# A queue of its own for the retention of a diffusion layer, and pooled differences written in place

## The chip, the cores and the metric

The kernel runs on one core of one Trainium2 chip, as one launch. The metric is the device time of that launch in microseconds (us), the median of three runs.

## What is computed

Two layers of a hybrid backbone over 256 latent tokens and 256 context tokens, 1024 channels. Each layer normalises and modulates its input, projects it once, feeds three token mixers in parallel, and merges them behind sigmoid gates; a SwiGLU block follows. Layer 0 computes all 512 tokens. Layer 1 computes its outputs for the 256 latent tokens alone and takes only keys and values from the context.

```python
def _token_mixers(hx, hc, w_in, ...):
    ux = _split_cols(hx @ w_in)
    ...
    a_x = _na_latent(ux[0], ux[1], ux[2], k_na_c, v_na_c, rpb)
    ...
    o_rx, _, _ = _bi_retention(q_rx, k_rx, v_rx, lg_f, lg_b, s_f, s_b)
    r_x = _ret_out(o_rx, ux[6], gn_g)
    p_x = _pool_mixer(ux[7], pool_w, pool_scale)
    mix_x = _merge(a_x, r_x, p_x, ux[8], ux[9], ux[10], wpa, wpb, wpc, wo)

def _ret_out(o, g, gn_g):
    mu = jnp.mean(o, axis=-1, keepdims=True)
    var = jnp.mean(jnp.square(o - mu), axis=-1, keepdims=True)
    y = _merge_heads((o - mu) * lax.rsqrt(var + GN_EPS)) * gn_g.astype(jnp.float32)
    return (jax.nn.silu(g.astype(jnp.float32)) * y).astype(g.dtype)

def _pool_mixer(u, pool_w, pool_scale):
    # four groups of 128 channels, windows of 2, 4, 8 and 16 tokens
    groups.append(mean - uf[..., sl])
    ...
    y = jnp.einsum('bngc,gcd->bngd', pooled, pool_w).reshape(b, n, POOL_WIDTH)
    return y * pool_scale

def _merge(a, r, p, ga, gb, gc, wpa, wpb, wpc, wo):
    m = (jax.nn.sigmoid(ga) * (a @ wpa) + jax.nn.sigmoid(gb) * (r @ wpb)
         + jax.nn.sigmoid(gc) * (p @ wpc))
    return m @ wo
```

## The kernel before

Everything is kept channel by channel: a tile has 128 channels as partitions and tokens along its rows. Every fp32 operand of a large product is split into a high and a low part of fp32r, and a product is three matmuls (`mm3`, L189 to L191). The weights stream in as 138 chunks of 128x1024 per layer. A chunk is loaded to `raw` (SyncE), its high part is cast on ScalarE (`hl`, L117), its low part subtracted on VectorE (`hl`, L107). Chunks are prepared up to three ahead of their use.

Engines take their instructions in the order in which the Python code writes them; nothing reorders them. Three helper loops issue the dense matmuls: `tokmajor` (values, token by token), `fm` (everything else, one PSUM tile of tag `g`, four of which exist, for each block of 128 output channels), and `branch`. `branch` does one of the three gated branches: for each of four pairs of output blocks two gate products (24 matmuls each, evicted on ScalarE with a sigmoid, L1000) and two branch products (12 matmuls each, merged with the gate on VectorE, L1004 to L1007).

Small work is woven into the dense matmuls by Python generators in three queues: `lanes["attn"]`, `lanes["pool"]` and `lanes["rope"]`. Within `fm` and `tokmajor`, `tick()` (L146) moves the first generator of each queue on by one step. In layer 0 `fm` does so every 6 matmuls of 512 columns, in layer 1 every 12 matmuls of 256 columns; `tokmajor` every 6 of 512. `drain(name)` (L158) runs what is left of a queue with no dense matmul between. `pipeline(items, stride)` (L168) turns lists of stages into such a generator, two steps for each stage: first what runs on the other engines, then what runs on TensorE.

The mixer of a layer, in order: keys and queries of the attention; its values (CV); with the attention queued, the retention's keys and queries, the pool's input `up` (CU), the retention's values `rv` (CRV), the retention's gate `gt` (CG, four blocks); then branches A (attention), C (pool) and B (retention).

The pool mixer is `pool_task` (L773). For each of four groups it makes running sums on GpSimd (`pb`, one buffer, L803 and L812), then the difference of mean and input on VectorE into a new tile `pl` (L820), then a product with `pw` on TensorE (L780), and a scaled eviction on ScalarE back into `up` (L784). It is queued when CRV begins, but a flag `hold`, set during CRV, keeps the first difference from being issued until CRV has ended. As `pb` has one buffer, the sums of the next group wait for this difference. The products come in between, through a little timetable `late`.

The retention is made of `ret_item` (L889, for each of four heads: decay tables `dm`, scores `ps`, masked scores `sm`, output `po`, statistics), `ret_stack` (L865, casts of keys `rkd`, `rkl` and queries `rqs`) and `ret_fin` (L964, normalised output `y`, its transpose `pt` on TensorE, L977, product with the gate `gt`, L980). `pt` and `po` have one PSUM tile each. All of it goes into the queue `attn`, after CG and after `drain("attn")`:

```python
        items[0][0][0]()
        items[0][1][0]()
        items[0][0] = items[0][1] = (None, None)
        lanes["attn"].append(ret_stack())
        lanes["attn"].append(pipeline(items, 4 if both else 2))
        lanes["attn"].append(pipeline([ret_fin(hd) for hd in range(4)], 2))
```

Then come four Silu on `gt` (L1044), branch A, `drain("pool")`, branch C, `drain("attn")` and branch B, which needs the finished `gt`.

Of the kernel before, what the change touches and what calls it, by code (L numbers as in the profile page):

```python
# [8 lines left out]
F32 = mybir.dt.float32  # L9
# [23 lines left out]
def hybrid_dit_kernel(ctx: ExitStack, tc: tile.TileContext, hT, wst, adaf, crow_d, vec_d,  # L33
# [52 lines left out]
        return vec[:, l * V_L + off + i:l * V_L + off + i + 1]  # L86

    raw_t, hl_t = {}, {}
    st = {"dma": 0, "prep": 0, "half": 0, "credit": 0.0, "rate": 0.0, "cap": 10 ** 6, "hold": 0, "lazy": False}
    total = 2 * NCH  # L90

    def raw_tile():
# [16 lines left out]
    def prep_to(i, wait=False):  # L109
        if not wait:  # L110
            prep_lo(i)
        while st["prep"] <= min(i, total - 1):
            j = st["prep"]
            load_to(j)
            t = wp.tile([128, 2, 1024], F32R, name="hl", tag="hl", bufs=4)
            r = raw_t.pop(j)
            S.copy(t[:, 0], r)  # L117
            late.append((j, r, t))
            if not wait:
                prep_lo(i)  # L120
            hl_t[j] = t
            st["prep"] += 1
# [9 lines left out]
        load_to(i + 5)  # L132
        flush()

    lanes = {"attn": [], "pool": [], "rope": []}
    ada_q = []

    def step(q):
        while q:
            try:  # L140
                next(q[0])
                break
            except StopIteration:
                q.pop(0)

    def tick():  # L146
        step(lanes["pool"])
# [74 lines left out]
    def chunk8(j):  # L222
        return [(j, b) for b in range(8)]
# [344 lines left out]
    def mixer(l, mp, outs, u):  # L568
# [9 lines left out]
        def t2(name):  # L578
            return mp.tile([128, 512], F32, name=name, tag="t2", bufs=5)
# [42 lines left out]
        def ev_nak(i, c=ALL):  # L622
            def ev(o):
                for a, r in enumerate(rows):
                    S.copy(nakd[2 * i + a][r, c], o[r])
                for a, r in enumerate(rows):
                    hi = nakd[2 * i + a][r, c]
                    V.tensor_tensor(nakl[2 * i + a][r, c], o[r], hi.bitcast(F32), op=ALU.subtract)
                    P.tensor_copy(nakd[2 * i + a][rows[1 - a], c], hi)
            return ev  # L630

        def ev_naq(i):
            def ev(o):
# [139 lines left out]
        def pool_task():  # L773
            pw = sm.tile([128, 4, 128], F32, name="pw", tag="acc", bufs=1)
            nc.sync.dma_start(out=pw, in_=pw_d[l])
            late = {}

            def pmm(gi, o2):
                pp = pg()
                TE.matmul(pp[:, :nq], pw[:, gi], o2[:, :nq], start=True, stop=True)  # L780
                return pp

            def pev(gi, pp):
                S.activation(up[gi][:, :, 8:264], pp[:, :nq].rearrange("p (s t) -> p s t", t=256), AF.Copy,  # L784
                             scale=vcol(l, V_PS, gi))

            t = [0]

            def pause():
                t[0] += 1  # L790
                if t[0] in late:
                    gi, o2 = late.pop(t[0])
                    pp = pmm(gi, o2)
                    late[-t[0] - 1] = (gi, pp)
                elif -t[0] in late:
                    pev(*late.pop(-t[0]))

            for gi in range(4):
                b = mp.tile([128, 1 + so, 272], F32, name="pb", tag="pb", bufs=1)
                a, w = up[gi], 1  # L800
                for j in range(gi + 1):
                    n = 272 - 2 * w + 1
                    P.tensor_tensor(b[:, :, :n], a[:, :, :n], a[:, :, w:w + n], op=ALU.add)  # L803
                    a = b
                    w *= 2
                    yield
                    pause()
                s0 = 8 - w // 2
# [13 lines left out]
                late[t[0] + 4] = (gi, o2)  # L822
                yield
                pause()
            while late:
                yield
                pause()

        if both:
            for i in range(8):  # L830
                if i == 4:
                    prep_to(10)
                (ev_nak(i) if i < 4 else ev_naq(i - 4))(outs[i])
        else:
            for i, o in enumerate(outs):
                ev_nak(i)(o)
            n = len(outs)
            fm([(chunk8(base + CK + i), ev_nak(i)) for i in range(n, 4)], hn, ALL)
            fm([(chunk8(base + CQ + i), ev_naq(i)) for i in range(4)], hn, cq)
        if both:  # L840
            decay_logs(u)
        st["lazy"] = True
        lanes["attn"].append(pipeline(items, 1, (10 if both else 0)))
        tokmajor(base + CV, hn, nav)
        fm([(chunk8(base + CRK + i), ev_k(i)) for i in range(2)], hn, ALL)
        fm([(chunk8(base + CRQ + i), ev_q(i)) for i in range(2)], hn, cq)
        fm([(chunk8(base + CU + i), ev_u(i)) for i in range(4)], hn, cq)
        drain("rope")
        lanes["pool"].append(pool_task())
        st["hold"] = 1  # L850
        tokmajor(base + CRV, hn, rv)
        st["hold"] = 0
        fm([(chunk8(base + CG + i), ev_g(i)) for i in range(4)], hn, cq)
        drain("attn")
        st["lazy"] = False

        m = [mp.tile([128, 512], F32, name=f"m{i}", tag=f"nak{i}") for i in range(4)] + nav
# [106 lines left out]
        def ret_fin(hd):  # L964
# [17 lines left out]

            return [(None, None), (norm, None), (None, trans), (fin, None)]

        def msplit(ks):
            for k in ks:
                split([t[:, cq] for t in hn[k]], m[k][:, cl])
# [44 lines left out]
                bran(0)  # L1032
                bran(1)

        items = [ret_item(hd) for hd in range(4)]
        items[0][0][0]()
        items[0][1][0]()
        items[0][0] = items[0][1] = (None, None)
# [9 lines left out]
        drain("attn")  # L1048
        branch(base + CB, [gt[i] for i in range(4)], False, True)
        if both:  # L1050
            h_tiles()
# [297 lines left out]
```

## Time and profile before

| | |
|---|---|
| median of 3 runs | 1386.01 us (1384.87 to 1386.74) |
| the profiled execution | 1382.58 us, of which 1380.8 us span of instructions |
| TensorE busy with matmuls (PE) | 1322.7 us, 96% |
| VectorE (DVE), ScalarE (ACT), GpSimd (POOL) | 894.2, 597.2, 200.2 us |
| chain that ended last | PE 87%, DVE 8%, ACT 2% |
| DMA | 207.27 MB, mean 150 GB/s |

Times in the profile are counted from the start of the span. Layer 0's mixer ends at about 430 us, layer 1's runs from about 905 to 1150 us. In a row of the timeline the number in brackets is how long the engine had been idle, and what ended the idle time. In a row of the windows view, PEclk is the share of TensorE's full clock that was granted.

### The profile page before, as it was taken

To read this page: it belongs to the slowest core of one execution; us is meant where nothing else is said; L and a number is where in the kernel's file an instruction comes from. 1 tells how busy PE (TensorE), PEld (TensorE's weight loads), DVE (VectorE), ACT (ScalarE), POOL (GpSimd) and SP (SyncE) were. 2 spreads that over 40 slices of the span, in tenths; PEclk is the share of its full clock that TensorE was granted. 3 is DMA by queue.
4 is the path that set the end of the run, shared out by engine and by line. 5 is a ranking of instruction groups with operands and counts; after the bars stand their busy time and mean duration, and the time that the engine had idled before them with its cause. 6 is when DMAs were issued, how large, how long until landed. Compare 5 with 4: busy or idle time off the path is not lost.

```text
span 1380.8 us, 19738 instructions
## 1 busy us (share of the span) xinstructions
PE 1322.7 (96%) x7658; PEld 1147.2 (83%) x7658; DVE 894.2 (65%) x1467; ACT 597.2 (43%) x929; POOL 200.2 (14%) x230
## 2 busy tenths in 40 slices
PE   4799999899999999999999999999999989999997
PEld 2578777688888888888888888988889989899997
DVE  8997554766877766565555653665538877655555
ACT  5484554544232435232123232465556545544453
POOL 6652302412000001000000000142134200000000
PEclk9999999999999999999999999999999999999999
DMA  7433322433545624355445653243435665455553
GB/s 261 168 110 117 98 71 83 128 123 122 183 162 162 201 71 138 124 171 165 155 139 172 211 183 99 70 140 108 142 122 185 217 237 177 151 184 195 183 171 106
DMA packets 62304, 207.27 MB, mean 150 GB/s; under 512 B 7041, under 2 KB 11521, under 8 KB 62209
## 3 DMA queue, kind: packets, MB, share of 16 engines
q1 hardware_dynamic: 50546, 163.97, 36.3%
q10 hardware_dynamic: 11664, 42.04, 9.2%
q8 instruction: 60, 0.98, 0.3%
q14 instruction: 34, 0.28, 0.1%
HBM read 204.94 MB, written 1.05 MB: 149 GB/s over the span
## 4 chain that ended last, share of the span: by engine, by line
PE 87%; DVE 8%; ACT 2%; issue 2%; DMA 0%; POOL 0%; SPq 0%; DVEq 0%; ACTq 0%; POOLq 0%
PE pg L189 26%; PE pg L190 26%; PE pg L191 26%; PE po L941 1%; DVE hl L107 1%; DVE tmp L441 1%; PE pt L675 1%; PE po L687 1%; DVE mods L522 1%; PE ps L643 1%; PE ps L644 1%; DVE rkl L876 0%; ACT hl L117 0%; DVE acc L476 0%; ACT hh L310 0%
## 5 line engine op out<-in xcount | busy, mean ns | idle before, releaser
L189 PE MATMUL pg<-hh,hl 128*128 128x256 f32 (+1 forms) x1568 | 530.9, 339 | 15.2 <-ACT hh L516 12.7
L191 PE MATMUL pg<-hl,hl 128*128 128x256 f32 (+1 forms) x1568 | 527.4, 336 | 2.2 <-DVE hl L542 1.6
L190 PE MATMUL pg<-hh,hl 128*128 128x256 f32 (+1 forms) x1568 | 526.2, 336 | 1.4 <-DVE hl L107 1.4
L107 DVE TENSOR_TENSOR hl<-raw,hl 128x1024 fp32r<-128x1024 f32 x276 | 342.3, 1244 | 174.8 <-ACT hl L117 169.8
L117 ACT CAST hl<-raw 128x1024 fp32r<-128x1024 f32 x276 | 287.6, 1046 | 207.5 <-PE pg L191 108.0
L189 PEld LDWEIGHTS pg<-hh,hl 128*128 128x128 f32 x1568 | 302.0, 193 | 48.7 <-ACT hh L516 15.1
L191 PEld LDWEIGHTS pg<-hl,hl 128*128 128x128 f32 x1568 | 301.7, 192 | 34.6 <-DVE hl L542 4.3
L190 PEld LDWEIGHTS pg<-hh,hl 128*128 128x128 f32 x1568 | 301.9, 193 | 32.1 <-DVE hl L107 2.1
L378 DVE CUSTOM_DVE_ANT_0 tmp<-ada,cb 128x1024 bf16<-128x1024 f32 x128 | 156.1, 1226 | 27.1 <-DMA ada<-in_adaf 17.8
L189 PE MATMUL pg<-fh,hl 128*128 128x256 f32 (+1 forms) x374 | 121.6, 325 | 0.0
L190 PE MATMUL pg<-fh,hl 128*128 128x256 f32 (+1 forms) x374 | 121.4, 325 | 0.0
L191 PE MATMUL pg<-fl,hl 128*128 128x256 f32 (+1 forms) x374 | 121.4, 325 | 0.0
L319 POOL TENSOR_TENSOR hl<-tmp,hh 128x256 fp32r<-128x256 f32 x20 | 14.8, 738 | 627.4 <-ACT hh L308 371.1
L291 ACT CAST fh<-sg 128x512 fp32r<-128x512 f32 (+1 forms) x44 | 22.6, 513 | 140.9 <-DVE sg L1150 140.9
L190 PEld LDWEIGHTS pg<-fh,hl 128*128 128x128 f32 x374 | 70.1, 188 | 7.2
L189 PEld LDWEIGHTS pg<-fh,hl 128*128 128x128 f32 x374 | 70.1, 187 | 7.1
L191 PEld LDWEIGHTS pg<-fl,hl 128*128 128x128 f32 x374 | 70.1, 187 | 7.1
L335 DVE SCALAR_TENSOR_TENSOR h<-pg,mods,h 128x256 f32<-128x256 f32 x72 | 32.7, 480 | 65.8 <-PE pg L191 65.7
L1150 DVE TENSOR_TENSOR sg<-pg,sg 128x512 f32<-128x512 f32 (+1 forms) x44 | 24.5, 557 | 51.1 <-PE pg L191 47.7
L1000 ACT ACTIVATE tmp<-pg 128x512 f32<-128x512 f32 (+1 forms) x48 | 23.5, 490 | 77.2 <-PE pg L191 76.2
L1147 ACT ACTIVATE sg<-pg 128x512 f32<-128x512 f32 (+1 forms) x44 | 21.6, 491 | 69.2 <-PE pg L191 69.2
L189 PE MATMUL pg<-hl,hh 128*128 128x512 f32 x128 | 50.6, 395 | 0.0
(241 smaller groups left out, 1643.4 us busy)
## 6 DMA issues: line engine op xcount, KB each, us to landing
raw<-in_wst SPq DMA_DIRECT2D x276, 512.0 KB, 3.6
ada<-in_adaf ACTq DMA_DIRECT2D x80, 512.0 KB, 3.8
wa<-in_adaf SPq DMA_DIRECT2D x16, 512.0 KB, 4.5
h<-in_hT SPq DMA_DIRECT2D x16, 256.0 KB, 5.0
bm<-in_bias SPq DMA_DIRECT2D x32, 128.0 KB, 2.0
out<-yt SPq DMA_DIRECT2D x4, 256.0 KB, 2.8
cs<-in_rope SPq DMA_DIRECT2D x2, 256.0 KB, 3.0
pw<-in_pw SPq DMA_DIRECT2D x2, 256.0 KB, 3.6
```

Source lines behind the costliest of these rows:

```text
L107: V.tensor_tensor(t[:, 1], r, t[:, 0].bitcast(F32), op=ALU.subtract)
L117: S.copy(t[:, 0], r)
L189: TE.matmul(o, wh, xh, start=a, stop=False)
L190: TE.matmul(o, wl, xh, start=False, stop=False)
L191: TE.matmul(o, wh, xl, start=False, stop=z)
L291: S.copy(d0, src)
L319: P.tensor_tensor(hn[k][1][:, c], t[:, c], hi, op=ALU.subtract)
L335: V.scalar_tensor_tensor(h[k][:, c], o, mods[l][:, col + k, s:s + 1], h[k][:, c], op0=ALU.mult, op1=ALU.add)
L378: V.tensor_tensor_reduce(out=tmp().bitcast(BF16), in0=tiles[n], in1=cb[s], scale=1.0, scalar=0.0, op0=ALU.mult, op1=ALU.add, accum_out=mod ...
L1000: S.activation(sg[f][:, cl], o, AF.Sigmoid)
L1147: S.activation(e["s"][:, c], o, AF.Silu)
L1150: V.tensor_tensor(e["s"][:, c], o, e["s"][:, c], op=ALU.mult)
```

## The change

There is a fourth queue, `lanes["ret"]`. `tick()` moves it on whenever the queue `attn` is empty. It holds one generator, `ret_lane`, queued at the start of CRV: the first head's decay, `ret_stack`, a wait for the end of `hold`, the heads' pipeline, a wait for a flag `gated`, then `ret_fin`. The four Silu follow `drain("attn")` directly and set `gated`. Branch B is preceded by `drain("ret")`.

The pool's difference is written into `up` itself, over its own input. `hold` no longer stands ahead of it, so sums and differences of all four groups are issued one after the other from the start of CRV, with two steps between the last sum and the difference. All four products and evictions follow when `hold` has ended, a product every second step; the timetable `late` is gone.

```diff
@@ tick
-        step(lanes["attn"])
+        step(lanes["attn"] or lanes["ret"])
@@ pool_task
+            ov = [t[:, :, 8:264] for t in up]
...
+            def pmm(gi):
                 pp = pg()
-                TE.matmul(pp[:, :nq], pw[:, gi], o2[:, :nq], start=True, stop=True)
+                TE.matmul(pp[:, :nq], pw[:, gi], ov[gi], start=True, stop=True)
                 return pp
...
-                for _ in range(4):
-                    yield
-                    pause()
-                while st["hold"]:
-                    yield
-                o2 = t2("pl")
-                ov = o2[:, :nq].rearrange("p (s t) -> p s t", t=256)
-                V.scalar_tensor_tensor(ov, b[:, :, s0:s0 + 256], 1.0 / w, up[gi][:, :, 8:264],
+                yield
+                yield
+                V.scalar_tensor_tensor(ov[gi], b[:, :, s0:s0 + 256], 1.0 / w, ov[gi],
                                        op0=ALU.mult, op1=ALU.subtract)
-                late[t[0] + 4] = (gi, o2)
                 yield
-                pause()
-            while late:
+            while st["hold"]:
                 yield
-                pause()
+            for gi in range(4):
+                pp = pmm(gi)
+                yield
+                pev(gi, pp)
+                yield
@@ mixer
+        def ret_lane():
+            items = [ret_item(hd) for hd in range(4)]
+            items[0][0][0]()
+            items[0][1][0]()
+            items[0][0] = items[0][1] = (None, None)
+            yield
+            yield from ret_stack()
+            while st["hold"]:
+                yield
+            yield from pipeline(items, 4 if both else 2)
+            while not st["gated"]:
+                yield
+            yield from pipeline([ret_fin(hd) for hd in range(4)], 2)
...
         lanes["pool"].append(pool_task())
         st["hold"] = 1
+        lanes["ret"].append(ret_lane())
         tokmajor(base + CRV, hn, rv)
         st["hold"] = 0
         fm([(chunk8(base + CG + i), ev_g(i)) for i in range(4)], hn, cq)
         drain("attn")
+        for i in range(4):
+            S.activation(gt[i], gt[i], AF.Silu)
+        st["gated"] = True
         st["lazy"] = False
...
-        lanes["attn"].append(ret_stack())
-        lanes["attn"].append(pipeline(items, 4 if both else 2))
-        lanes["attn"].append(pipeline([ret_fin(hd) for hd in range(4)], 2))
         st["rate"] = 0.75 if both else 0.45
-        for i in range(4):
-            S.activation(gt[i], gt[i], AF.Silu)
         branch(base + CA, None, True)
         drain("pool")
         branch(base + CC, [up[i][:, :, 8:264] for i in range(4)], False)
-        drain("attn")
+        drain("ret")
+        st["gated"] = False
         branch(base + CB, [gt[i] for i in range(4)], False, True)
```

How the instructions move, at three places.

TensorE in layer 0, the fourth group's product (L780; `pl` is the new tile of before, `up` the input). Before it stands behind the first pair of branch A (`naq` is the attention's output):

```order
L191 MATMUL pg<-naq_677,hl 128x512
L189 MATMUL pg<-naq_678,hl 128x512
L190 MATMUL pg<-naq_678,hl 128x512
L191 MATMUL pg<-naq_679,hl 128x512
L780 MATMUL pg<-pl,pw 128x512
L189 MATMUL pg<-hh_85,hl 128x512
L190 MATMUL pg<-hh_85,hl 128x512
```

Now, at the start of the last block of CG:

```order
L189 MATMUL pg<-hh_99,hl 128x512
L190 MATMUL pg<-hh_99,hl 128x512
L191 MATMUL pg<-hl_100,hl 128x512
L780 MATMUL pg<-up_683,pw 128x512
L189 MATMUL pg<-hh_85,hl 128x512
```

It has moved ahead of the whole first pair of branch A, and its difference on VectorE has moved from between the retention's casts (`rqs`) to well ahead of them. The retention's own matmuls stand where they stood in layer 0.

TensorE in layer 1, the retention's last transposes (L977, now L933). Before, two heads' transposes stand together (two each) at the end of branch C, ahead of branch B:

```order
L190 MATMUL pg<-br_8846,hl 128x256
L191 MATMUL pg<-br_8847,hl 128x256
L977 MATMUL pt<-ident,y 128x128 x4
L189 MATMUL pg<-hh_85,hl 128x256
L190 MATMUL pg<-hh_85,hl 128x256
```

Now only the last head's two stand there; the third head's stand 48 dense matmuls earlier:

```order
L190 MATMUL pg<-hh_99,hl 128x256
L191 MATMUL pg<-hl_100,hl 128x256
L933 MATMUL pt<-ident,y 128x128 x2
L189 MATMUL pg<-hh_85,hl 128x256
...
L191 MATMUL pg<-br_8868,hl 128x256
L933 MATMUL pt<-ident,y 128x128 x2
L189 MATMUL pg<-hh_85,hl 128x256
```

ScalarE in layer 1, from the last copy of CG's gate to the first two sigmoids of branch A (L1000, now L1003). Before (`dm` is the first head's decay, L903 to L905):

```order
L619 COPY gt_8245<-pg 128x256
L903 ACTIVATE dm<-dtab,lg_84 128x384
L904 ACTIVATE tmp<-dtab,lg_84 128x384
L905 ACTIVATE dm<-dm 128x384
L1044 ACT_TABLE_LOAD
...
L871 CAST rkd_8271<-rk_6985 64x512
L871 CAST rkd_8288<-rk_6985 64x512
L117 CAST hl<-raw 128x1024
L1000 ACT_TABLE_LOAD
L1000 ACTIVATE tmp<-pg 128x256
```

Now:

```order
L619 COPY gt_8289<-pg 128x256
L983 ACT_TABLE_LOAD
...
L841 CAST rqs<-rq_6983 64x256
L784 ACTIVATE up_7014<-pg,vec 128x256
L841 CAST rqs<-rq_6983 64x256
L117 CAST hl<-raw 128x1024
L1003 ACT_TABLE_LOAD
L1003 ACTIVATE tmp<-pg 128x256
```

The decay and the key casts have moved ahead of the last copy, into CG; two query casts and one eviction of a pool product have come in. The number of table loads is the same, 26.

## Rows read from the trace of the kernel before

**Rows 1.** The page, part 1: busy time, share of the span, instructions.
```profile
PE 1322.7 (96%) x7658; PEld 1147.2 (83%) x7658; DVE 894.2 (65%) x1467; ACT 597.2 (43%) x929; POOL 200.2 (14%) x230
```
**Rows 2.** Waits of TensorE, whole span: us in total, times, longest.
```profile
PE pt L977 <- DVE y L970: 3.8, 1, 3.8
PE pg L780 <- DVE pl L820: 3.5, 1, 3.5
PE pg L189 <- ACT tmp L1000: 3.1, 4, 1.1
PE po L941 <- DVE sm L923: 2.0, 1, 2.0
```
**Rows 3.** Timeline of TensorE, layer 0, branch A: start, us, instruction [idle before].
```profile
262.52 2.05 PE L780 MATMUL pg<-pl,pw 128*128 128x512 f32 x2 [3.54 <-DVE pl L820]
263.58 1.42 PE L189 MATMUL pg<-hh,hl 128*128 128x512 f32 x1
...
268.21 0.48 PE L189 MATMUL pg<-hh,hl 128*128 128x512 f32 x1
```
**Rows 4.** Windows: stretch, us, busy of PE, PEld, DVE, ACT, POOL; PEclk, DMA.
```profile
262.52:268.21 5.69, 5.69 (x12) 3.79 (x13) 5.16 (x7) 1.85 (x3) 0.00 (x0) 0.50 0.80 257
```
**Rows 5.** Timeline of VectorE, layer 0, the fourth group's difference.
```profile
261.68 0.69 DVE L820 SCALAR_TENSOR_TENSOR pl<-pb,up 128x512 f32<-128x512 f32 x1
```
**Rows 6.** Timeline of GpSimd: layer 0's fourth group; layer 1's third and fourth.
```profile
251.19 2.18 POOL L812 TENSOR_TENSOR pb<-pb,icnt 128x8 f32<-128x8 f32 x4
...
1026.86 0.64 POOL L803 TENSOR_TENSOR pb<-up 128x271 f32<-128x271 f32 x1
...
1043.83 3.96 POOL L803 TENSOR_TENSOR pb<-pb 128x269 f32<-128x269 f32 x3
```
**Rows 7.** Timeline of TensorE, layer 0, a pool product that did not wait.
```profile
233.74 1.02 PE L780 MATMUL pg<-pl,pw 128*128 128x512 f32 x2
...
234.82 0.39 PE L190 MATMUL pg<-hh,hl 128*128 128x512 f32 x1
235.05 0.40 PE L191 MATMUL pg<-hl,hl 128*128 128x512 f32 x1
```
**Rows 8.** Timeline of ScalarE: a gate's copy in layer 0; layer 1, CG to branch A.
```profile
236.17 0.59 ACT L619 COPY gt<-pg 128x512 f32<-128x512 f32 x1 [3.90 <-PE pg L191]
...
1024.24 0.37 ACT L619 COPY gt<-pg 128x256 f32<-128x256 f32 x1 [1.56 <-PE pg L191]
...
1026.23 1.28 ACT L1044 ACT_TABLE_LOAD   x1
1027.53 1.34 ACT L1044 ACTIVATE gt<-gt 128x256 f32<-128x256 f32 x4
1028.77 1.24 ACT L871 CAST rkd<-rk 64x512 fp32r<-64x512 f32 x2
...
1031.11 1.28 ACT L1000 ACT_TABLE_LOAD   x1
1032.41 0.38 ACT L1000 ACTIVATE tmp<-pg 128x256 f32<-128x256 f32 x1
```
**Rows 9.** Timeline of TensorE, layer 1, end of branch C and start of branch B.
```profile
1116.22 0.66 PE L977 MATMUL pt<-ident,y 128*128 128x128 f32 x2 [3.75 <-DVE y L970]
1116.53 0.56 PE L189 MATMUL pg<-hh,hl 128*128 128x256 f32 x1
...
1121.89 0.28 PE L190 MATMUL pg<-hh,hl 128*128 128x256 f32 x1
1122.01 0.28 PE L191 MATMUL pg<-hl,hl 128*128 128x256 f32 x1
```
**Rows 10.** Windows, as rows 4, layer 1, after the wait of rows 9.
```profile
1116.20:1121.90 5.70, 5.68 (x28) 5.69 (x29) 4.32 (x9) 1.41 (x3) 0.00 (x0) 0.52 0.22 70
```
**Rows 11.** Timeline of VectorE, layer 1, behind branch C's merges.
```profile
1115.34 0.48 DVE L980 SCALAR_TENSOR_TENSOR gt<-pt,vec,gt 128x256 f32<-128x256 f32 x1
1115.73 0.59 DVE L970 TENSOR_SCALAR y<-y,mv,gr 128x128 f32<-128x128 f32 x2
```

More of the change, by code (lines that the diff above doesn't have):

```diff
@@ L88, in hybrid_dit_kernel @@
     raw_t, hl_t = {}, {}
-    st = {"dma": 0, "prep": 0, "half": 0, "credit": 0.0, "rate": 0.0, "cap": 10 ** 6, "hold": 0, "lazy": False}
+    st = {"dma": 0, "prep": 0, "half": 0, "credit": 0.0, "rate": 0.0, "cap": 10 ** 6, "hold": 0, "gated": False, "lazy": False}
     total = 2 * NCH
@@ L133, in use @@
         flush()
-    lanes = {"attn": [], "pool": [], "rope": []}
+    lanes = {"attn": [], "pool": [], "rope": [], "ret": []}
     ada_q = []
@@ L775, in pool_task @@
             nc.sync.dma_start(out=pw, in_=pw_d[l])
-            late = {}
-            def pmm(gi, o2):
+            ov = [t[:, :, 8:264] for t in up]
+            def pmm(gi):
                 pp = pg()
-                TE.matmul(pp[:, :nq], pw[:, gi], o2[:, :nq], start=True, stop=True)
+                TE.matmul(pp[:, :nq], pw[:, gi], ov[gi], start=True, stop=True)
                 return pp
             def pev(gi, pp):
-                S.activation(up[gi][:, :, 8:264], pp[:, :nq].rearrange("p (s t) -> p s t", t=256), AF.Copy,
+                S.activation(ov[gi], pp[:, :nq].rearrange("p (s t) -> p s t", t=256), AF.Copy,
                              scale=vcol(l, V_PS, gi))
[L787 to L796, printed above, removed]
             for gi in range(4):
@@ L812, in pool_task @@
                         P.tensor_tensor(b[:, s, c], b[:, s, c], icnt[:, gi, e], op=ALU.mult)
-                for _ in range(4):
-                    yield
-                    pause()
-                while st["hold"]:
-                    yield
-                o2 = t2("pl")
-                ov = o2[:, :nq].rearrange("p (s t) -> p s t", t=256)
-                V.scalar_tensor_tensor(ov, b[:, :, s0:s0 + 256], 1.0 / w, up[gi][:, :, 8:264],
+                yield
+                yield
+                V.scalar_tensor_tensor(ov[gi], b[:, :, s0:s0 + 256], 1.0 / w, ov[gi],
                                        op0=ALU.mult, op1=ALU.subtract)
-                late[t[0] + 4] = (gi, o2)
                 yield
-                pause()
-            while late:
+            while st["hold"]:
                 yield
[L827 to L853, printed above, removed]
-        drain("attn")
-        st["lazy"] = False
-        m = [mp.tile([128, 512], F32, name=f"m{i}", tag=f"nak{i}") for i in range(4)] + nav
+            for gi in range(4):
[3 more added lines that the diff above has]
+                yield
         tts = range(4) if both else range(2, 4)
@@ L983, in ret_fin @@
             return [(None, None), (norm, None), (None, trans), (fin, None)]
+        def ret_lane():
[11 more added lines that the diff above has]
+            yield from pipeline([ret_fin(hd) for hd in range(4)], 2)
+        if both:
+            for i in range(8):
+                if i == 4:
+                    prep_to(10)
+                (ev_nak(i) if i < 4 else ev_naq(i - 4))(outs[i])
+        else:
+            for i, o in enumerate(outs):
+                ev_nak(i)(o)
+            n = len(outs)
+            fm([(chunk8(base + CK + i), ev_nak(i)) for i in range(n, 4)], hn, ALL)
+            fm([(chunk8(base + CQ + i), ev_naq(i)) for i in range(4)], hn, cq)
+        if both:
+            decay_logs(u)
+        st["lazy"] = True
+        lanes["attn"].append(pipeline(items, 1, (10 if both else 0)))
+        tokmajor(base + CV, hn, nav)
+        fm([(chunk8(base + CRK + i), ev_k(i)) for i in range(2)], hn, ALL)
+        fm([(chunk8(base + CRQ + i), ev_q(i)) for i in range(2)], hn, cq)
+        fm([(chunk8(base + CU + i), ev_u(i)) for i in range(4)], hn, cq)
+        drain("rope")
+        lanes["pool"].append(pool_task())
+        st["hold"] = 1
+        lanes["ret"].append(ret_lane())
+        tokmajor(base + CRV, hn, rv)
+        st["hold"] = 0
+        fm([(chunk8(base + CG + i), ev_g(i)) for i in range(4)], hn, cq)
+        drain("attn")
+        for i in range(4):
+            S.activation(gt[i], gt[i], AF.Silu)
+        st["gated"] = True
+        st["lazy"] = False
+        m = [mp.tile([128, 512], F32, name=f"m{i}", tag=f"nak{i}") for i in range(4)] + nav
         def msplit(ks):
@@ L1033, in branch @@
                 bran(1)
[L1035 to L1038, printed above, removed]
-        lanes["attn"].append(ret_stack())
-        lanes["attn"].append(pipeline(items, 4 if both else 2))
-        lanes["attn"].append(pipeline([ret_fin(hd) for hd in range(4)], 2))
         st["rate"] = 0.75 if both else 0.45
-        for i in range(4):
-            S.activation(gt[i], gt[i], AF.Silu)
         branch(base + CA, None, True)
@@ L1047, in mixer @@
         branch(base + CC, [up[i][:, :, 8:264] for i in range(4)], False)
-        drain("attn")
+        drain("ret")
+        st["gated"] = False
         branch(base + CB, [gt[i] for i in range(4)], False, True)
```

## The prediction, made before the changed kernel was run

> **What bounds the kernel now.** I read the page first: TensorE is busy in 96% of the span [rows 1], so 1380.8 less 1322.7, 58 us, is all the idle time there is, and no edit on another engine counts unless it takes away a TensorE wait. So the next view was what TensorE waited for. Four rows of it come from the pool mixer and the retention, the code that the change touches [rows 2]: one wait of 3.8 us for the retention's normalised head `y`, one of 3.5 us for a pool difference `pl`, four together of 3.1 us for ScalarE's gate sigmoids, and one of 2.0 us for masked scores `sm`. The other rows of that view lie in the start and in the norms, which stay as they are.
>
> Then I looked at what stands around each wait in TensorE's own timeline. The wait for `pl` is in layer 0, in branch A. Matmuls behind it start 0.43 us apart instead of the 0.23 us of an undisturbed stretch [rows 3, 7]; the granted clock there is 0.50, that is 1.2 instead of 2.4 GHz [rows 4]. The reader should see that the idle time is about half of the loss. The wait for `y` is in layer 1, at the join of branches C and B, and again the clock falls behind it, to 0.52 [rows 9, 10]. The shorter waits, of 2.0 and at most 1.1 us each [rows 2], I count at their idle time alone.
>
> **The pool change, layer 0.** The fourth product stands behind branch A's first pair, and its difference began on VectorE at 261.68 us [rows 5]. GpSimd had finished that group's sums at 251.19 + 2.18 = 253.4 us [rows 6]. So the sums were not late: the difference stood 8.3 us in VectorE's queue behind the retention's casts. In the change it stands ahead of them, and the product stands 96 matmuls earlier. This wait should go. Its worth: TensorE was idle from 262.52 - 3.54 = 258.98 us, and back at full clock at 268.21 [rows 3], 9.23 us in all. At full clock the work in that stretch is the product and the first matmul behind it, 234.82 - 233.74 = 1.08 us as for the product that did not wait [rows 7], and 8 more matmuls at 0.23 us, 1.84 us. The loss is 9.23 - 2.92 = 6.3 us.
>
> A new wait takes some of it back. There are four PSUM tiles of tag `g`. The fourth product is now issued first thing in CG's last block, and the tile that comes round to it is that of CG's third block, which TensorE has only just finished. Its copy on ScalarE takes 0.59 us [rows 8], and the hand-overs add to it. I take 0.9 us, with bounds of 0 (the copy hidden) and 1.2 us (two such copies). Layer 0: 6.3 - 0.9 = **5.4 us**.
>
> The other edits of the pool cost nothing of their own: eight differences, twenty sums, eight products and eight evictions remain, of the same sizes; they only start sooner. What hides them is the attention's and CRV's dense work; a rival below says what happens if it does not.
>
> **The queue of the retention, layer 0.** The attention's queue empties only a step or two before the end of CG, so the retention's matmuls stay where they were. Only the first decay moves ahead of the last gate copy. I count nothing; ScalarE had idled 3.90 us ahead of a gate's copy in CG [rows 8], which covers it.
>
> **The queue of the retention, layer 1.** Here the attention ends some 8 steps before CG does, and the retention gains most of these. Before, the last steps were left for the drain: the fourth head's transposes needed `pt`, which the third head still held until its product with the gate at 1115.34 us, and their own `y` at 1115.73 [rows 11], both in VectorE's queue behind merges. In the change 48 dense matmuls lie between the two heads' transposes, so both instructions have 5.8 us. The wait should go. Its worth: idle from 1116.22 - 3.75 = 1112.47 us, full clock by 1122.01 [rows 9], 9.54 us. Work in it: two transposes, 0.31 us, and 26 matmuls, 28 instructions with the transposes [rows 10], at 0.12 us, 3.1 us. The loss is 9.54 - 3.43 = **6.1 us**. If that cover is gone, what is late next is branch B's first operand, the split of `gt`; it has 48 gate matmuls of cover, as before.
>
> The wait of 2.0 us for `sm` [rows 2]: the retention's heads have new neighbours, the pool products no longer run between them, and between scores and output there are again 48 matmuls. It may vanish or reappear. Bounds 2.0 and 0; I take half, **1.0 us**.
>
> The sigmoids, 3.1 us in four waits [rows 2]. From the last gate copy to the first sigmoid it takes 1032.41 - 1024.24 = 8.2 us [rows 8]. Out of this go the decay, some 1.6 us between that copy's end and the first table load, and two key casts, 1.24 us [rows 8]. Two query casts and one eviction come in, at most half of 1.24 us each, so 1.9 us. The sigmoid is 1 to 2 us sooner. But all four products now take `g` tiles, so branch A's first product waits for the first sigmoid where before it was the second product, 12 matmuls or 1.4 us later. The two cancel: 0. Bounds: the whole 3.1 us gained; or, if TensorE idles longer here by another 1.1 us, the longest of the four, and the clock falls as it did at the join, where 26 matmuls took 5.5 instead of 3.1 us [rows 9, 10], 1.1 + 2.4 = 3.5 us lost.
>
> A table load takes 1.28 us and the next activation starts 1.30 us after it began [rows 8]. The Trainium skill, "ScalarE: Activation LUTs", section "What ACT_TABLE_LOAD costs", gives about 2.66 us for a switch, drain included, and its rules for kernel authors say to group work by table; that speaks against decays between Silu and sigmoid. By that price the two loads ahead of the first sigmoid would cost an estimated 2.8 us more, and the sum would be 9.7 instead of 12.5 us. The trace does not bear it out, as its 1.30 us includes everything up to the next activation.
>
> **The sum.** 5.4 + 6.1 + 1.0 + 0 = 12.5 us. Against the profiled execution's own time, 1382.58 us, this gives 1370.1 us. That execution was 3.4 us below the median of the runs, 1386.01 us; the same gain from the median gives **1373.5 us**.
>
> **The rivals.**
>
> *ScalarE becomes the bound in layer 1's first pair.* For it: its queue already holds TensorE up four times, and the query casts now stand ahead of the sigmoids and wait for VectorE in turn. Against it: the first sigmoid comes sooner. The 3.5 us above are given back: 1377.
>
> *The last transposes still wait.* The queue does not do what it says in layer 1 if the third head's product with the gate comes late behind branch C's merges. For it: in the rows before, exactly these merges held it [rows 11]. Against it: 48 matmuls of cover. Left are 5.4 + 1.0 us: 1379.6.
>
> *VectorE gives it all back.* TensorE arrives 6 us sooner at what follows, while VectorE was busy 5.16 of 5.69 us behind the first wait [rows 4]. If low parts of weights or merges are then the last to arrive, the waits only move: 1386. Against it: chunks are prepared three ahead, and none of TensorE's waits in the branches is for them.
>
> *Everything goes.* The new tile wait stays hidden, and sigmoid and `sm` waits vanish: 6.3 + 6.1 + 2.0 + 3.1 = 17.5 us, 1368.5.
>
> *Slower: VectorE stands still in the attention.* Eight differences now stand between the softmax instructions, and VectorE, which works in order, waits at each until GpSimd has that group's sums. GpSimd's sums slow down: 0.64 us for one, 1.32 for each of three that ran while VectorE worked [rows 6]. The Trainium skill, "GPSIMD Engine Reference", section "Specifications", says that the two share their access to SBUF; the rows agree. A fourth group then needs 4 x 1.32 + 2.18 = 7.5 us. It has six steps from its first sum to its difference, each at least 6 matmuls of 0.23 us or 12 of 0.12, so 8.3 us. Should GpSimd fall behind that, and TensorE run out of prepared chunks, each stop would cost as much as the one in layer 0, 6.3 us. From the second on the gain is gone; three stops cost 18.9 us: 1392.4. Against it: GpSimd is busy 14% of the span [rows 1], and the bias additions of the attention are through before the sums begin.
>
> **How the numbers follow.** Chances: forecast 0.56; ScalarE the bound 0.16; everything goes 0.10; last transposes still wait 0.07; VectorE gives it back 0.06; slower 0.05. A measurement of this kernel can tell about 0.2%, 2.8 us, from no change. The first four cases are all faster by more: 0.89. Given back is no change, 0.06; slower 0.05. The range runs from 1368 us, where everything goes, to 1380 us, where the last transposes still wait; left out are the last two cases and the edges.
>
> **What would show it.** Right: no wait of TensorE for the pool's difference and none above 1 us for `y`; no stretch at half clock near 260 us or at the join of branches C and B; a new wait of about 0.9 us for ScalarE at a pool product in layer 0's CG. Wrong: a half-clock stretch in branch A of layer 1, idle VectorE behind GpSimd within the attention, or new TensorE waits for low parts of weights after 260 us.

## The result, and the profile after

The changed kernel takes **1368.53 us** (median of 4 runs, 1367.34 to 1370.24), the kernel before, run beside it, 1385.67 us (4 runs). The ratio is 0.9874, with a 95% interval of 0.9862 to 0.9886: 17.1 us less. The profiled executions differ by less, 1382.58 and 1370.24 us, because TensorE waited 4.6 us for `acc` at the start in the one of before, and about 8 us in that of after and in nearly all others below. Times by position are therefore compared within a stretch, not from the span's start.

Busy times, the first part of the page of the changed kernel, which answer to [rows 1]:

```profile
PE 1317.3 (96%) x7658; PEld 1143.5 (84%) x7658; DVE 896.8 (66%) x1467; ACT 597.4 (44%) x929; POOL 189.4 (14%) x230
```

No instruction has gone. Of what TensorE waited for, in the changed kernel (us in total, times, longest), these rows answer to [rows 2]:

```profile
PE pg L189 <- ACT rv L242: 0.8, 1, 0.8
PE po L897 <- DVE sm L879: 0.6, 1, 0.6
```

The waits for `pl`, for `y` and for the sigmoids are gone, all three; `sm` is down from 2.0 to 0.6; a wait of 0.8 us for a copy of `rv` is new. At both places the half clock is gone too. The windows of the changed kernel in branch A of layer 0 and at the join of layer 1 (columns as in [rows 4]) have a PEclk of 1.00 where [rows 4, 10] had 0.50 and 0.52:

```profile
255.00:272.00 17.00, 17.00 (x79) 14.06 (x79) 15.07 (x20) 8.72 (x12) 1.34 (x2) 1.00 0.46 153
...
1100.00:1115.00 15.00, 15.00 (x130) 15.00 (x129) 13.86 (x25) 7.76 (x13) 0.00 (x0) 1.00 0.70 235
```

At the join, VectorE writes the last head's `y` (now L926), and TensorE transposes (L933), the third head first. VectorE, then TensorE, in the changed kernel:

```profile
1101.86 0.59 DVE L926 TENSOR_SCALAR y<-y,mv,gr 128x128 f32<-128x128 f32 x2
```

```profile
1099.91 0.38 PE L933 MATMUL pt<-ident,y 128*128 128x128 f32 x2
...
1105.75 0.38 PE L933 MATMUL pt<-ident,y 128*128 128x128 f32 x2
```

Between the two heads' transposes lie 5.84 us, and `y` is there 3.3 us early (1101.86 + 0.59 against 1105.75), where in [rows 9, 11] it was 3.75 us late.

To compare kernels by stretch I use **lost time**, worked out from the trace: for each matmul the time from its start to the next one's start, less the median of that time for its shape, summed. It holds waits and half clock together. Even an undisturbed stretch has some, so only differences count.

| lost time, us | layer 0, 205 to 275 us | layer 1, 905 to 1005 | 1005 to 1050 | 1050 to 1130 |
|---|---|---|---|---|
| before | 9.9 | 1.5 | 5.1 | 8.4 |
| changed | 4.4 | 1.5 | 1.1 | -0.1 |

That is 5.5 us in layer 0, 4.0 around the sigmoids, 8.5 with `sm` and `y`: 18.0 us, against 17.1 by the medians. Of the 8.5, the loss reckoned for `y` (6.1) and the shorter wait for `sm` (1.4) make 7.5; the last 1 us is not placed.

### The profile page after: what moved, and what is told of

It reads as the page before. It is cut to its first block, busy times and chain, and to the rows that moved or that the text cites. A ratio compares the mean times of both kernels' runs of the same rounds, so it can differ in the third digit from the quotient of the medians.

```text
span 1368.4 us, 19732 instructions
## 1 busy us (share of the span) xinstructions
PE 1317.3 (96%) x7658; PEld 1143.5 (84%) x7658; DVE 896.8 (66%) x1467; ACT 597.4 (44%) x929; POOL 189.4 (14%) x230
## 4 chain that ended last, share of the span: by engine, by line
PE 88%; DVE 7%; ACT 2%; issue 2%; DMA 0%; SPq 0%; DVEq 0%; ACTq 0%
PE pg L189 27%; PE pg L191 27%; PE pg L190 27%; PE po L897 1%; PE pt L675 1%; PE po L687 1%; DVE tmp L441 1%; DVE hl L107 1%; DVE mods L522 1%; PE ps L643 1%; PE ps L644 1%; ACT hl L117 1%; DVE acc L476 1%; DMA h<-in_hT 0%; PE pg L780 0%
## 5 line engine op out<-in xcount | busy, mean ns | idle before, releaser
L1003 ACT ACTIVATE tmp<-pg 128x512 f32<-128x512 f32 (+1 forms) x48 | 23.6, 491 | 71.4 <-PE pg L191 66.1
```

The costliest lines, as they stand in the source:

```text
L1003: S.activation(sg[f][:, cl], o, AF.Sigmoid)
```

## The sigmoids: what the traces show

The prediction let two effects cancel here. ScalarE of the changed kernel in layer 1 (the sigmoid is now L1003), and TensorE at the first product that takes the first sigmoid's tile:

```profile
1023.59 0.37 ACT L619 COPY gt<-pg 128x256 f32<-128x256 f32 x1 [0.71 <-PE pg L191]
...
1028.80 1.28 ACT L1003 ACT_TABLE_LOAD   x1
1030.09 0.38 ACT L1003 ACTIVATE tmp<-pg 128x256 f32<-128x256 f32 x1
...
1036.59 0.38 ACT L1003 ACTIVATE tmp<-pg 128x256 f32<-128x256 f32 x1 [0.40 <-PE pg L191]
```

```profile
1030.01 0.59 PE L780 MATMUL pg<-up,pw 128*128 128x256 f32 x2
1030.53 0.39 PE L189 MATMUL pg<-naq,hl 128*128 128x256 f32 x1
```

Counted from the last gate copy, the first sigmoid begins after 6.50 us instead of 8.17 [rows 8]: 1.67 us sooner, within the 1 to 2 us forecast. The need comes only 0.58 us sooner: before, TensorE arrived at 1032.84 - 1.08 = 1031.76 us (TensorE before, below), 7.52 us after the copy; now 1030.53 - 1023.59 = 6.94.

```profile
1032.84 0.39 PE L189 MATMUL pg<-naq,hl 128*128 128x256 f32 x1 [1.08 <-ACT tmp L1000]
```

The forecast was 1.4 us. The 12 matmuls are indeed gone from in front, but two more pool products of some 0.4 us stand in the stretch. So the sigmoid, done at 1030.47, is just in time.

The two later waits have another cause. ScalarE before:

```profile
1038.07 0.41 ACT L885 CAST rqs<-rq 64x256 fp32r<-64x256 f32 x1 [1.48 <-DVE rkl L876]
1039.49 0.40 ACT L885 CAST rqs<-rq 64x256 fp32r<-64x256 f32 x1 [1.01 <-DVE rkl L876]
1042.38 0.41 ACT L885 CAST rqs<-rq 64x256 fp32r<-64x256 f32 x1 [2.49 <-DVE rqs L886]
...
1043.77 0.38 ACT L1000 ACTIVATE tmp<-pg 128x256 f32<-128x256 f32 x1
```

ScalarE stood three times for VectorE, with the third sigmoid queued behind. In the changed kernel these casts are done by 1032 us and the third sigmoid waits for TensorE (1036.59, above) instead of the other way round.

## The experiments

Ratios are to the kernel before, run beside each; medians of 4 to 11 runs.

| kernel | median, us | ratio, 95% interval | lost time, us, in the four stretches |
|---|---|---|---|
| pool task alone | 1382.97 | 0.9985 [0.9976, 0.9995] | 4.5, 2.5, 4.5, 9.5 |
| retention's queue alone | 1368.61 | 0.9885 [0.9872, 0.9899] | 4.9, 1.6, 0.9, 0.3 |
| changed, casts late | 1380.37 | 0.9966 [0.9954, 0.9978] | 4.8, 1.7, 2.5, 10.6 |
| changed, heads late | 1374.82 | 0.9923 [0.9911, 0.9936] | 4.7, 1.5, 0.8, 6.4 |
| early decay alone | 1379.98 | 0.9957 [0.9944, 0.9969] | 4.8, 1.4, 3.3, 9.5 |
| queue alone, decay late | 1376.52 | 0.9934 [0.9920, 0.9947] | 9.9, 2.4, 4.3, -0.7 |
| changed, no gap | 1369.14 | 0.9879 [0.9866, 0.9893] | 3.7, 1.6, 0.6, 0.4 |
| changed, gap of four | 1367.21 | 0.9868 [0.9854, 0.9881] | 3.5, 1.6, 1.4, -0.9 |

The stretches are cut by time, so a wait near an edge can fall in or out. The 2.5 and 2.4 in the second one are such a case: a wait of 0.9 us for a low part stands near 905 us in the kernel before too, and in these two kernels it falls inside.

### The pool task alone

The kernel before with the new `pool_task`, nothing else.

```diff
-                while st["hold"]:
-                    yield
-                o2 = t2("pl")
...
+                V.scalar_tensor_tensor(ov[gi], b[:, :, s0:s0 + 256], 1.0 / w, ov[gi],
+                                       op0=ALU.mult, op1=ALU.subtract)
```

> The kernel before with the new pool task alone: differences written in place and issued in CRV without the hold, all four products from CG on; the retention is queued behind CG as before. Theory (each half of the change has a gain of its own, and the sigmoid waits go because the retention's casts leave branch A): only layer 0's wait for the pool difference goes, 6.3 us, less 1.0 us for the new wait for the copies of rv: 5.3 us faster than before, about 1380.4 us; the wait of 3.8 us for y at the join and the half clock behind it stay; the four sigmoid waits of layer 1 stay, 3 to 4.5 us with their restarts. Rival (the sigmoid waits go because the pool's differences and evictions leave branch A): these go here already, 9.8 us faster, about 1376 us, and no sigmoid wait in layer 1's branch A.

Measured: 2.4 us faster (0.7 to 3.3), less than either. Up to 275 us layer 0 gains 5.4 us of lost time as the theory had it. Some of it is given back at the masked scores `sm`: just behind that stretch, at 277.44 us, TensorE waits 1.7 us for them, and in layer 1 3.0 us. TensorE's waits:

```profile
PE po L926 <- DVE sm L908: 3.2, 2, 3.0
PE pt L962 <- DVE y L955: 3.2, 1, 3.2
...
PE pg L190 <- DVE hl L107: 2.5, 4, 1.1
PE pg L189 <- ACT tmp L985: 2.0, 1, 2.0
...
PE ps L897 <- DVE sm L908: 1.7, 1, 1.7
```

The first sigmoid now costs one wait of 2.0 us instead of two of 1.08 and 0.82: all products take `g` tiles, so the need is sooner while the sigmoid is not. The loss of 3.5 us that the prediction had bounded for this case did not come: the stretch has 4.5 us of lost time against 5.1 before. The later two sigmoid waits are gone, though the casts still stand in branch A; a wait of 1.1 us for a low part (`hl`) has come instead. The rival falls, as the first sigmoid is still late; but for the later two it was partly right, and the forecast that all four stay was wrong.

### The retention's queue alone

The changed kernel with `pool_task` of before.

```diff
-                V.scalar_tensor_tensor(ov[gi], b[:, :, s0:s0 + 256], 1.0 / w, ov[gi],
-                                       op0=ALU.mult, op1=ALU.subtract)
...
+                while st["hold"]:
+                    yield
+                o2 = t2("pl")
```

> The changed kernel with the pool task of before: the retention has its own queue that follows the attention, the pool keeps its hold, its own tile and its products in branch A. Theory: layer 1's wait for y goes (6.1 us with the half clock), the sigmoid waits go (4.5 us) and the wait for the masked scores shrinks (1.4 us): 12.0 us faster than before, about 1373.7 us; layer 0's wait of 3.5 us for the pool difference stays, with its half clock. Rival (the sigmoid waits belong to the pool's instructions): 7.5 us faster, about 1378 us, with 3 us of sigmoid waits left in layer 1.

Measured: 1368.61 us, the whole gain. Both theories had left layer 0 as before, and both were wrong there. TensorE and then ScalarE of this kernel in layer 0, and the window behind the wait:

```profile
262.48 1.10 PE L780 MATMUL pg<-pl,pw 128*128 128x512 f32 x2 [1.23 <-DVE pl L820]
```

```profile
243.91 0.59 ACT L619 COPY gt<-pg 128x512 f32<-128x512 f32 x1 [1.73 <-PE pg L191]
244.52 1.28 ACT L998 ACT_TABLE_LOAD   x1
```

```profile
262.00:268.00 6.00, 5.52 (x25) 4.34 (x26) 5.31 (x8) 2.28 (x3) 0.00 (x0) 1.00 0.78 256
```

Difference and product stand where they stood, but the wait is 1.23 us instead of 3.54 [rows 3], and the clock does not fall. From the start of the last gate copy to the table load it takes 0.61 us instead of 2.21: the first head's decay, which lay between them, has moved ahead of the copy. ScalarE before, at the same place:

```profile
241.63 0.59 ACT L619 COPY gt<-pg 128x512 f32<-128x512 f32 x1 [3.35 <-PE pg L191]
...
243.84 1.28 ACT L1044 ACT_TABLE_LOAD   x1
```

That led to the next two runs.

### The early decay alone

The retention's queue alone, with all but the first decay held until Silu: the retention is then as late as before the change.

```diff
-            yield from ret_stack()
-            while st["hold"]:
+            while not st["gated"]:
                 yield
+            yield from ret_stack()
             yield from pipeline(items, 4 if both else 2)
-            while not st["gated"]:
-                yield
```

> The pool task of before and the retention as late as before; of the change only this is left: the first head's decay is issued in CG, ahead of the last copies of gt, instead of behind them. Theory A (in layer 0 the wait for the pool difference hangs on the chain last copy, decay, Silu, key casts, query casts, difference; without the decay in it the difference comes some 2 us sooner relative to TensorE, the wait falls to 1.2 us and the clock does not fall): 5 us of layer 0 are gained by this alone, and the first two sigmoid waits of layer 1, 2.4 us; join, later sigmoid waits and sm wait stay: 7.5 us faster than before, about 1378 us. Theory B (the decay is worth only its own 1.6 us, the rest of layer 0's gain in the run with the retention's queue alone came from its steps): about 1383 us, with the half clock in layer 0 still there.

Measured: 6.0 us faster. Layer 0 decides for theory A: 4.8 us lost instead of 9.9, a wait of 1.2 us, and the clock stays:

```profile
PE pg L189 <- ACT tmp L1016: 2.5, 4, 0.7
PE po L912 <- DVE sm L894: 2.0, 1, 2.0
...
PE pg L780 <- DVE pl L820: 1.2, 1, 1.2
```

```profile
262.00:268.00 6.00, 4.79 (x19) 3.31 (x19) 5.26 (x7) 2.35 (x4) 0.00 (x0) 1.00 0.62 185
```

The forecast of 7.5 us was 1.5 us too high: the sigmoid waits fall only from 3.1 to 2.5 us, and behind the wait for `sm` the clock falls, which it did not before (last section).

### The queue alone, the decay late

```diff
-            items[0][0][0]()
-            items[0][1][0]()
-            items[0][0] = items[0][1] = (None, None)
...
         drain("attn")
+        ritems[0][0][0]()
+        ritems[0][1][0]()
+        ritems[0][0] = ritems[0][1] = (None, None)
         for i in range(4):
             S.activation(gt[i], gt[i], AF.Silu)
```

> The retention's queue with the pool task of before, but the first decay back at its place between the last copy of gt and the four Silu; casts and heads stay early. Theory A: layer 0's wait for the pool difference and the half clock behind it come back, 5 us slower than the run with the retention's queue alone, and in layer 1 the first sigmoid is up to 1.6 us later: about 1373.5 to 1375.5 us. Theory B: 1369 to 1370.5 us, clock 1.0 in layer 0's branch A.

Measured: 1376.52 us, by the ratios 6.8 us slower than the queue alone (by the medians 7.9), 1 us above theory A. A wait of TensorE in layer 0; TensorE and VectorE in layer 1; and the windows behind both waits:

```profile
PE pg L780 <- DVE pl L820: 3.5, 1, 3.5
```

```profile
1036.16 0.38 PE L190 MATMUL pg<-naq,hl 128*128 128x256 f32 x1 [1.72 <-DVE hl L107]
```

```profile
1033.98 0.87 DVE L857 TENSOR_TENSOR rqs<-rq,rqs 64x256 fp32r<-64x256 f32 x2 [4.73 <-ACT rqs L856]
```

```profile
1036.20:1040.50 4.30, 4.30 (x23) 4.30 (x24) 3.53 (x6) 4.12 (x9) 0.00 (x0) 0.60 0.75 236
...
266.40:272.10 5.70, 5.68 (x11) 3.80 (x12) 5.15 (x7) 1.87 (x3) 0.00 (x0) 0.50 0.75 254
```

Layer 0's wait is back to 3.5 us with its half clock, as theory A has it; that is 5.0 us of lost time. Layer 1 loses 3.4 us more between 1005 and 1050 us and gains 1.0 us behind. The cause there is not the sigmoid: VectorE, which works in order, stood 4.73 us at `rqs` for ScalarE's late casts and brought a low part of the weights 1.72 us late, and the clock fell behind it.

### Casts late, heads late

Casts late is the edit of the early decay alone, made on the changed kernel. Heads late:

```diff
             while st["hold"]:
                 yield
+            for _ in range(0 if both else 4):
+                yield
             yield from pipeline(items, 4 if both else 2)
```

> The changed kernel with the retention's casts of keys and queries, and all behind them, held until the four Silu are issued; only the first head's decay is still early. The retention is then as late in layer 1 as before the change. Theory: the sigmoid waits come back, the larger part of 4.5 us, and the four transposes at the join wait again, 6.1 us: 9 to 11 us slower than the changed kernel, about 1378.5 us. Rival (the first decay, early, is what freed the first sigmoid): no sigmoid waits, 6.1 us slower, about 1374.6 us. Rival (the pool alone freed the join and the sigmoids): no slower than the changed kernel.

> The changed kernel with four empty steps in layer 1 ahead of the retention's heads: casts stay early, the heads come 48 dense matmuls later, so that two heads' transposes stand together at the join again. Theory: only the wait for y and the half clock behind it come back, 6.1 us (5 to 7) slower than the changed kernel, about 1374.6 us, with a PEclk near 0.5 behind the join and no sigmoid waits. Rival (the wait for y comes from VectorE's and ScalarE's load by the casts in branches A and C, not from the place of the heads): the wait stays under 1 us, no slower by more than 1 us.

Heads late: 1374.82 us, 6.3 us slower than the changed kernel, as expected. TensorE at its join, and the window:

```profile
1108.70 0.66 PE L933 MATMUL pt<-ident,y 128*128 128x128 f32 x2 [3.19 <-DVE y L926]
```

```profile
1108.00:1114.00 6.00, 5.29 (x25) 5.31 (x26) 5.01 (x11) 1.76 (x3) 0.00 (x0) 0.50 0.26 89
```

So the place of the heads alone sets the wait at the join, and the casts do not. Casts late: 11.8 us slower, more than expected, and by other waits:

```profile
PE po L897 <- DVE sm L879: 4.4, 3, 2.9
PE pt L933 <- DVE y L926: 3.2, 1, 3.2
...
PE pg L190 <- DVE hl L107: 2.5, 4, 1.1
...
PE pg L189 <- ACT tmp L1001: 0.4, 1, 0.4
```

The join wait is back, but of the sigmoid waits only 0.4 us, as the rival on the early decay had it: the pool task alone, with the same late casts and a late decay, waits 2.0 us there. The late casts delay the masked scores instead. My theory that the casts in branch A are what the sigmoids wait for holds for the second pair only with the old pool task: the early decay alone, which has it, still waits 0.6 us at both later sigmoids; with the new one (pool task alone, casts late) these waits are gone, and 1.1 us is waited for `hl`. So either half of the change removes the later two, but only the early casts leave no wait in their place.

### The gap between sums and difference

The changed kernel with no step, or with four steps, where the change has two.

```diff
-                yield
-                yield
                 V.scalar_tensor_tensor(ov[gi], b[:, :, s0:s0 + 256], 1.0 / w, ov[gi],
                                        op0=ALU.mult, op1=ALU.subtract)
```

> The changed kernel without the two steps between the last sum and the difference, so that VectorE reaches each difference sooner than GpSimd has its sums. Theory (VectorE has room: in the changed kernel it stood 3.2 us for such sums in layer 1 and TensorE did not wait): VectorE's waits for pb grow, TensorE's do not by more than 1 us; within 2 us of the changed kernel, 1367 to 1370.5 us. Rival (the slower case of the prediction: VectorE standing in the attention's softmax stops TensorE): 3 to 19 us slower than the changed kernel, 1372 us or more, with new TensorE waits before 260 us.

> The changed kernel with four steps instead of two between the last sum and the difference. Theory (the new wait of 0.8 us for the copies of rv in layer 0 comes from the fourth group's sums, which run while the softmax ahead of these copies is on VectorE): the sums come six steps later, this wait goes, 1.0 us faster, about 1367.5 us; nothing else changes. Rival (the wait has to do with the order on ScalarE alone): it stays at 0.8 us. Second rival (the products now come late): they stand in layer 0's branch A as before the change, take turns with the sigmoids for the g tiles, and TensorE waits there, 1 to 3 us slower.

No gap: 1369.14 us, the same within the measurement. The longest wait of VectorE for a group's sums in layer 1, first without the gap, then in the changed kernel:

```profile
981.10 0.43 DVE L801 SCALAR_TENSOR_TENSOR up<-pb,up 128x256 f32<-128x256 f32 x1 [0.26 <-POOL pb L800]
```

```profile
1017.62 0.43 DVE L803 SCALAR_TENSOR_TENSOR up<-pb,up 128x256 f32<-128x256 f32 x1 [3.17 <-POOL pb L800]
```

VectorE's waits did not even grow: without the gap the longest is 0.26 us. The one long standstill, 3.17 us, is the changed kernel's own, and no TensorE wait came of it. The slower rival is off by far.

Gap of four: 1367.21 us, and the wait for `rv` is gone, as expected. VectorE and then GpSimd of the changed kernel, behind them VectorE with the gap of four:

```profile
212.55 1.63 DVE L722 TENSOR_SCALAR p<-p,rs 128x256 f32<-128x256 f32 x2
...
214.81 0.62 DVE L711 TENSOR_SCALAR mx<-mx 128x2 f32<-128x2 f32 x1
```

```profile
211.78 3.62 POOL L792 TENSOR_TENSOR pb<-pb 128x538 f32<-128x538 f32 x3
```

```profile
210.85 0.62 DVE L722 TENSOR_SCALAR p<-p,rs 128x256 f32<-128x256 f32 x2
...
212.10 0.17 DVE L711 TENSOR_SCALAR mx<-mx 128x2 f32<-128x2 f32 x1
```

While GpSimd sums, the same softmax instructions take 1.63 and 0.62 us instead of 0.62 and 0.17. They stand ahead of the copies of `rv` through ScalarE, and TensorE's next tile is one of these. Lost time in layer 0 falls by 0.9 us. Without the gap the sums are over before these instructions, which take 0.62 and 0.17 us there, and the wait for `rv` is gone as well. The Trainium skill, "GPSIMD Engine Reference", section "Specifications", says that GpSimd and VectorE contend where VectorE's instructions have two inputs in SBUF or run in a mode that uses two ports. The rows agree that GpSimd's sums slow VectorE; which of the two cases this is, no run here shows.

### The changed kernel, the queue alone and the gap of four, side by side

> The changed kernel once more, as the measure for the next two on the same chip: 1368.5 us, 17 us faster than before.

> The retention's queue with the pool task of before. Theory (each half takes away layer 0's wait for the pool difference, and the queue alone takes away all in layer 1): within 1.5 us of the changed kernel. Rival (the pool's half adds what it gained alone, 2.4 us): 2 us or more slower than the changed kernel.

> The changed kernel with four steps between the last sum and the difference. Theory: 1.0 us faster than the changed kernel (the wait for the copies of rv) and up to 0.8 us more (the wait for sm), 1367 us. Rival: the medians lie within 0.5 us of each other.

Measured on one chip, 5 runs each: 1369.03 (1368.39 to 1369.15), 1368.88 (1368.50 to 1370.14) and 1366.18 us (1365.94 to 1366.50); ratios to before 0.9881, 0.9882 and 0.9862. The pool's half adds nothing to the queue. The gap of four is 2.85 us faster than the changed kernel, all its runs below all of the other's; it is the fastest version found. That is more than the 1.0 to 1.8 us expected: in the two profiles the four stretches differ by 1.6 us of lost time, and 1.5 us lie ahead of 100 us, where nothing was edited. So no more than the 1.6 us is shown to come from the gap.

## Why the prediction was right, and where not

**The total.** 1373.5 us was predicted and 1368.5 measured: the sign was right, and the range held by 0.5 us at its lower edge. The time is that of the rival in which everything goes, but that it meets it so closely is luck: that sum had 6.3 us for layer 0, 3.1 for the sigmoids and 2.0 for `sm`, and 5.5, 4.0 and 1.4 came. The gain of 17.1 us was 4.6 us above the forecast of 12.5; nearly all of that is the sigmoids.

**Layer 0, the wait for the difference.** 6.3 less 0.9, 5.4 us; measured 5.5 us of lost time. The pool task alone takes the wait away as described, but the net size was right in part by luck, as the next point shows. The prediction also gave it to the pool alone, and of the retention's queue in layer 0 it said "I count nothing", because the moved decay was covered at its new place. That step failed: it asked what the decay costs where it goes, not what is released where it leaves. The early decay alone is worth 5.1 us in layer 0. Either half removes this loss, and so together they gain it once.

**The new wait of 0.9 us.** It did not come. TensorE and ScalarE of the changed kernel at the fourth product:

```profile
242.15 1.02 PE L780 MATMUL pg<-up,pw 128*128 128x512 f32 x2
```

```profile
242.34 0.59 ACT L619 COPY gt<-pg 128x512 f32<-128x512 f32 x1 [2.01 <-PE pg L191]
```

The product starts before the third block's copy does, so its tile was another one. The assumption that the four tiles go round in turn was wrong: in the built program this product has the bank of CG's second block, copied at 233.88 us. A wait of nearly the same size, 0.8 us for `rv`, came at a place that the prediction had not looked at, so that the 0.9 us stood in the sum for the wrong wait.

**Layer 1, the join.** 6.1 us; the run with late heads puts back 6.3. Right in mechanism and size.

**The masked scores.** 1.0 us within 0 to 2.0; 2.0 became 0.6, 1.4 us gained. The wait is 0 to 1.2 us in every run with the casts early and 2.0 to 4.4 us in every run with the casts late, so it was the casts, more than the heads' new neighbours, that set it.

**The sigmoids.** "The two cancel: 0" was the mis-sized term. It measured 4.0 us of lost time, above the bound of 3.1 us, which left out some 0.3 us of restart with each wait. Two things were wrong: the two added products in TensorE's way were not counted, which makes the need 0.6 instead of 1.4 us sooner; and four waits were argued from the first, though the later two came from the casts in ScalarE's queue and went with either half of the change.

**Table loads.** In the changed kernel the sigmoid starts 1.29 us after its table load begins (1028.80 and 1030.09, above), with a weight cast just ahead and Silu before that. The trace again does not bear out the switch price of about 2.66 us in the Trainium skill, "ScalarE: Activation LUTs", section "What ACT_TABLE_LOAD costs".

**The rivals.** ScalarE as the bound shows in the pool task alone as a 2.0 us wait in the first pair, without a net loss there; the early decay keeps it away. The transposes did not wait, and VectorE did not give the gain back. VectorE stood once for GpSimd, 3.17 us, and TensorE did not wait for it.

## What to carry to other kernels

When an instruction leaves an in-order queue, price what stood behind it: the whole chain comes sooner, which can be worth more than the instruction (1.6 us of decay, 5 us of TensorE). When two parts of a change touch the same wait, its gain counts once; run each part alone before crediting either. And when an instruction that takes a tile is moved, count its own time into the arrival of what follows, and look up which tile it really gets.

## What the runs showed that was not expected

The clock does not follow the length of a wait alone. It stayed behind 1.23 us (the queue alone) and behind 1.98 us (the pool task alone, row and windows below), and fell behind 1.72 us (decay late, above).

```profile
1034.39 0.38 PE L189 MATMUL pg<-naq,hl 128*128 128x256 f32 x1 [1.98 <-ACT tmp L985]
```

```profile
1032.00:1036.00 4.00, 2.02 (x16) 1.62 (x16) 2.37 (x3) 3.92 (x7) 0.94 (x3) 1.00 0.27 53
1036.00:1040.00 4.00, 4.00 (x35) 3.93 (x34) 2.99 (x4) 2.94 (x5) 0.53 (x1) 1.00 0.68 245
```

The wait for `sm` was 1.96 us in two kernels. Before, the clock stayed; with the early decay alone it fell, to 0.67 in the window behind. Before, then early decay alone:

```profile
1074.00:1078.00 4.00, 2.32 (x20) 2.33 (x21) 2.46 (x9) 3.19 (x5) 0.15 (x1) 1.00 0.77 253
1078.00:1082.00 4.00, 4.00 (x36) 4.00 (x35) 3.49 (x7) 3.97 (x8) 0.87 (x1) 1.00 0.34 121
```

```profile
1076.00:1080.00 4.00, 4.00 (x25) 4.00 (x25) 3.40 (x7) 3.97 (x8) 0.94 (x1) 0.67 0.36 123
```

What sets it apart stays open; no run was made for it. In this kernel a wait between 1.7 and 2 us may cost little more than its length or nearly 2 us more: around the wait for `sm` 2.2 us of time are lost before and 3.8 with the early decay alone (1070 to 1082 us). The waits of 3.2 us and above at the join and in layer 0 all brought the half clock, and cost 1.4 to 3 us more than their length. At the join, against the changed kernel between 1090 and 1130 us, the same wait of 3.19 us cost 6.0 us with late heads and 4.6 to 5.0 us with the pool task alone, the early decay alone and casts late.
